# Two output tiles of the first pointwise layer beside the channel steps, in a one-core conformer trunk

## The chip, the core and the metric

The kernel runs on one core of one Trainium2 chip. The metric is the device time of one execution in microseconds (us); the median of three runs stands for a kernel. A separate execution, recorded by the hardware profiler, gives the profile. Engines are named as the profile does: PE is the matrix engine (PEld its weight loads), DVE the vector engine, ACT the scalar engine, POOL the general one, SP the engine that issues the DMAs.

## The reference

With depth 1 the trunk is one conformer layer and one gated conv-FFN for 1024 positions of width 1024, in float32:

```python
mod = silu(c) @ mod_w + mod_b                       # six vectors of 1024
sh_m, sc_m, gt_m, sh_f, sc_f, gt_f = split(mod, 6)
h = rmsnorm(x, norm_pre_mix) * (1 + sc_m) + sh_m
a, gt = split(h @ a_pw1_w + a_pw1_b, 2)             # pointwise 1
u = causal_dwconv(a * sigmoid(gt), a_dw_w) + a_dw_b # 31 taps
u = silu(layernorm(u)) 
y = u @ a_pw2_w + a_pw2_b
x = x + gt_m * rmsnorm(y, norm_post_mix)
...                                                 # the gated conv-FFN
```

## The kernel before

Positions are cut into two blocks of 512, channels into eight tiles of 128 (k for input channels, j for output channels). Every product of pointwise 1 is made from operands split into a high and a low part: `split` writes the high part (ACT, or DVE) and then the low part (DVE, or POOL), and `mm3` (lines 257 to 259) multiplies high by high, high by low and low by high. So one step of one k on one output tile is six matmuls of 512 columns, three for each of the two halves of the gated unit, and an output tile is 48.

The start of the program (lines 757 to 776) works in this order. `load_norm(0)` loads the four 128-row tiles of the first block of x, squares each on ACT (line 283), takes the root on POOL and scales on DVE (line 285). `pw1_weights(0, DV)` loads the two weight tiles of output tile 0 and splits them. `channel_vectors(k)` loads the 16 tiles of 512 KB of the modulation weights (`mod_ch`), two for each k. Then the loop over k runs four things, one step apart: `channel_partials` (line 150, eight small matmuls a chunk against silu(c), then a copy on ACT at line 154), `channel_sums` (line 159, then two small DVE operations that give the shift and scale of channel tile k), `modulate_T` (four transposes at line 266, the modulation on ACT at line 268, the split on DVE), and `pw1_step` of the k before, for output tile 0 alone. `glu` and the first tap of `conv` close tile 0. Output tiles 1 to 7 follow as whole tiles (`pw1`), each from hT, the eight modulated tiles that stay in SBUF. `load_norm(1)`, the second block of x, stands behind tile 1, and `modulate_block`, its eight times four transposes, behind tile 2.

What sets the order: each engine runs a fixed list in order, which a scheduler makes at build time from the program and from its own estimate of times. Loads go out on SP in its list's order, and at most eight are under way. Buffers are few and rotate: three `raw` tiles for loaded weights, four `W` tiles for split weights, eight `Y` tiles, six PSUM banks (`bank`) and two more (`cbank`) that the channel partials and the convolution share. A transfer or an operation that reuses a buffer waits for its last reader.

Of the kernel before, what the change touches and what calls it, by code (L numbers as in the profile page):

```python
# [8 lines left out]
F32 = mybir.dt.float32  # L9
F32R = mybir.dt.float32r  # L10
AF = mybir.ActivationFunctionType
ALU = mybir.AluOpType
# [3 lines left out]
P = 128  # L16
# [3 lines left out]
KD = D // P  # L20
# [27 lines left out]
def trunk_kernel(ctx, tc, x, vec, rows, mod_ch, mod_hp, w1, w2, wup, wdn, out):  # L48
# [19 lines left out]
    def nm(s):  # L68
        uid[0] += 1
        return f"{s}_{uid[0]}"  # L70

    def bank():
        return ps.tile([P, 512], F32, tag="bank", name=nm("bank"))
# [7 lines left out]
    def tAf():  # L81
        return pa.tile([P, 2, 512], F32, tag="A", name=nm("Af"))
# [7 lines left out]
    def tY():  # L90
        return py.tile([P, 1024], F32, tag="Y", name=nm("Y"))
# [8 lines left out]
    def V(name, i, n=1):  # L100
        o = _OFF[name] + i
        return v[:, o:o + n]
# [20 lines left out]

    cz = cst.tile([P, KD, 32], F32, name="cz")
    nc.gpsimd.memset(cz, 0.0)
    nc.scalar.activation(cz[:, :, 0], V("c", 0, KD), AF.Silu)
    sh_m = cst.tile([P, KD], F32, name="sh_m")
    s_m = cst.tile([P, KD], F32, name="s_m")
    sh_f = cst.tile([P, KD], F32, name="sh_f")
# [7 lines left out]
    def channel_vectors(k):  # L137

        ws = []
        for g in range(2):  # L140
            w = tAf().rearrange("p a b -> p (a b)") if k > 1 else tY()
            dma[0] = nc.sync.dma_start(w, mod_ch[k, g])
            ws.append(w)
        return ws
# [100 lines left out]
            hi.tensor_copy(dst[:, 0], src)  # L245
        split_lo[0] = lo.tensor_tensor(dst[:, 1], src, dst[:, 0].bitcast(F32), op=ALU.subtract)  # L246

    def weights(src, lo=nc.gpsimd):
        raw = pr.tile([P, 1024], F32, tag="raw", name=nm("raw"))
        dma[0] = nc.sync.dma_start(raw, src)  # L250
        w = pw.tile([P, 2, 1024], F32R, tag="W", name=nm("W"))
        split(w, raw, lo=lo)
        return w
# [35 lines left out]
    u = [[None] * KD for _ in range(NB)]  # L289
    tail = cst.tile([P, KD, PAD], F32, name="tail")  # L290

    def pw1_weights(j, lo=nc.gpsimd):
        return weights(w1[j], lo), weights(w1[KD + j], lo)

    def pw1_step(bks, ws, h, k):
        sl = slice(k * P, (k + 1) * P)
        for o, w in zip(bks, ws):
            mm3(o, (w[:, 0, sl], w[:, 1, sl]), (h[:, 0], h[:, 1]), k == 0, k == KD - 1)
# [457 lines left out]

    G, DV = nc.gpsimd, nc.vector
    hT = [[None] * KD for _ in range(NB)]
    xs = load_norm(0)
    ws = pw1_weights(0, DV)  # L760
    chunk = [channel_vectors(k) for k in range(KD)]
    issue = ctx.enter_context(ExitStack())
    issue.enter_context(tc.issue_after(dma[0].ins))

    bks = [bank(), bank()]
    part = [channel_partials(chunk[0])]
    for k in range(KD + 1):
        if k + 1 < KD:
            part.append(channel_partials(chunk[k + 1]))
        if k < KD:  # L770
            channel_sums(k, *part[k])
            hT[0][k] = modulate_T(xs, s_m, sh_m, k)
        if k > 0:
            pw1_step(bks, ws, hT[0][k - 1], k - 1)
    glu(0, 0, bks)
    cs0 = [conv(0, 0, POOL_TAPS)]

    loaded, parts = [], []

# [11 lines left out]
            p, h = todo.pop(0)  # L791
            loaded.append((p, h, piece_loads(p, h)))

    for j in range(1, KD):
        ws = pw1_weights(j)
        pw1(0, j, ws)
        if j == 2:
            with tc.issue_after(dma[0].ins):
                b2, g_f = spread(2, "b2"), spread(4, "g_f")
                g_m, early_m, use_m = into_rows(0, 3, "g_m")  # L800
            into = [(early_m, use_m), (None, into_channels(fin_sh)), (None, into_channels(fin_s))]
            todo = [(p, h) for p in range(3) for h in range(2)]
        if j == 1:
            xs = load_norm(1)
        if j == 2:
            hT[1] = modulate_block(xs, s_m, sh_m, nc.scalar, G)
        if j >= KD - 2:
            pieces()
        cs0.append(conv(0, j, POOL_TAPS))
        if j >= SHARED:  # L810
            pw1(1, j, ws)
            if j >= KD - 2:
                pieces()
# [130 lines left out]
```

## Time and profile before

| | us |
|---|---|
| median of three runs | 1091.83 (1091.65 to 1094.43) |
| the profiled execution, whole | 1093.15 |
| its span in the trace | 1091.4 |
| PE busy in it | 1063.2 |
| all other engines | 819.1 (DVE) or less |

The span is the traced part of the profiled execution; 1.75 us lie around it. PE's busy time includes modelled ends of matmuls, so it is read from the distance between starts rather than from the share. The trace rows give the start, the length, the engine, the line and operation, and in brackets how long the engine had been idle and what ended that. In the first 60 us the loads keep the DMA engines busy from about 5 us to 50 us.

### The profile page before, as it was taken

Reading aid. Unit: us, or ns where it says so; the run is one execution under the profiler, and the core shown is the slowest. Engines: PE = TensorE matmul, PEld = TensorE weight load, DVE = VectorE, ACT = ScalarE, POOL = GpSimd, SP = SyncE. Lnnn points to the kernel's source line nnn. Section 1 sums busy time; section 2 is a strip of 40 time slices with the busy share of each in tenths; the row PEclk is TensorE's granted clock in tenths of the full one; section 3 lists DMA queues with packets and bytes.
Section 4 is the critical chain, followed back from the end, with each engine's and each line's share of the span. In section 5 each row is a group of like instructions: output and inputs, shape, how many; then the busy total and the mean of one; then the engine's idle time right before and its main releaser. Section 6 shows DMA issues by size and latency. Waiting matters only on the chain.

```text
span 1091.4 us, 13051 instructions
## 1 busy us (share of the span) xinstructions
PE 1063.2 (97%) x4786; PEld 842.1 (77%) x4786; DVE 819.1 (75%) x1111; ACT 500.3 (46%) x774; POOL 515.5 (47%) x412
## 2 busy tenths in 40 slices
PE   5999999999899999999999999999999999999996
PEld 3778876778688888888887688888887888878884
DVE  3489989533799999989987683786587456965588
ACT  3495455452644544333444442445445344443443
POOL 1398876534734444444444453423247023650464
PEclk9999999999899999999999999999999999999998
DMA  9951135433422233342243343567214322033122
GB/s 367 374 189 63 41 134 193 155 127 106 145 71 93 96 97 97 97 174 92 97 140 115 96 144 92 179 201 281 91 37 154 116 97 91 19 122 117 39 75 80
DMA packets 41832, 139.01 MB, mean 127 GB/s; under 512 B 4644, under 2 KB 4644, under 8 KB 41768
## 3 DMA queue, kind: packets, MB, share of 16 engines
q1 hardware_dynamic: 41768, 138.18, 37.1%
q8 instruction: 37, 0.61, 0.2%
q14 instruction: 27, 0.22, 0.1%
HBM read 129.77 MB, written 8.39 MB: 127 GB/s over the span
## 4 chain that ended last, share of the span: by engine, by line
PE 85%; DVE 7%; POOL 2%; ACT 2%; issue 2%; DMA 1%; SPq 0%; DVEq 0%; ACTq 0%; POOLq 0%
PE bank L257 26%; PE bank L258 25%; PE bank L259 25%; DVE W L246 1%; DVE R L692 1%; PE bank L629 1%; PE bank L630 1%; PE bank L628 1%; PE bank L266 1%; PE bank L179 1%; DMA Y<-in_mod_ch 1%; DVE Y L474 1%; ACT W L243 1%; PE cbank L150 1%; DVE yacc L657 1%
## 5 line engine op out<-in xcount | busy, mean ns | idle before, releaser
L257 PE MATMUL bank<-A,W 128*128 128x512 f32 x960 | 378.8, 397 | 0.3 <-ACT U L268 0.3
L258 PE MATMUL bank<-A,W 128*128 128x512 f32 x960 | 378.5, 395 | 0.0
L259 PE MATMUL bank<-A,W 128*128 128x512 f32 x960 | 378.2, 395 | 0.0
L246 POOL TENSOR_TENSOR W<-raw,W 128x1024 fp32r<-128x1024 f32 x99 | 242.6, 2452 | 273.1 <-ACT W L243 231.1
L354 DVE SCALAR_TENSOR_TENSOR cbank<-U,vecs,cbank 128x512 f32<-128x512 f32 x424 | 290.8, 749 | 8.8 <-ACT cbank L342 7.6
L257 PEld LDWEIGHTS bank<-A,W 128*128 128x128 f32 x960 | 180.7, 189 | 48.1 <-DVE cbank L354 1.7
L259 PEld LDWEIGHTS bank<-A,W 128*128 128x128 f32 x960 | 180.8, 188 | 43.0 <-issue 0.8
L258 PEld LDWEIGHTS bank<-A,W 128*128 128x128 f32 x960 | 180.9, 188 | 42.7 <-issue 1.1
L243 ACT ACTIVATE W<-raw 128x1024 fp32r<-128x1024 f32 x150 | 158.0, 1054 | 109.7 <-PE bank L259 72.4
L527 ACT ACTIVATE U<-bank,vecs 128x512 f32<-128x512 f32 x88 | 68.4, 778 | 192.3 <-PE bank L259 191.9
L528 DVE SCALAR_TENSOR_TENSOR U<-bank,vecs,U 128x511 f32<-128x511 f32 x88 | 65.4, 745 | 78.5 <-ACT U L527 78.3
L257 PE MATMUL bank<-W,A 128*128 128x512 f32 x304 | 121.1, 398 | 0.0
L258 PE MATMUL bank<-W,A 128*128 128x512 f32 x304 | 120.1, 395 | 0.0
L259 PE MATMUL bank<-W,A 128*128 128x512 f32 x304 | 119.0, 395 | 0.0
L533 POOL TENSOR_TENSOR U<-U,hv 128x2 f32<-128x2 f32 x44 | 13.7, 312 | 154.6 <-DVE U L528 151.7
L246 DVE TENSOR_TENSOR W<-raw,W 128x1024 fp32r<-128x1024 f32 x51 | 62.2, 1221 | 16.3 <-ACT W L243 16.3
L246 DVE TENSOR_TENSOR A<-U,A 128x512 fp32r<-128x512 f32 x73 | 67.2, 932 | 8.2 <-ACT A L243 7.7
L352 POOL TENSOR_TENSOR Q<-Q,Q 128x512 f32<-128x512 f32 x48 | 62.2, 1296 | 15.9 <-ACT Q L348 14.9
L257 PEld LDWEIGHTS bank<-W,A 128*128 128x128 f32 x304 | 57.3, 188 | 13.6 <-DVE U L537 0.2
L258 PEld LDWEIGHTS bank<-W,A 128*128 128x128 f32 x304 | 57.3, 188 | 13.5 <-issue 0.5
L259 PEld LDWEIGHTS bank<-W,A 128*128 128x128 f32 x304 | 57.3, 188 | 13.3
L529 DVE SCALAR_TENSOR_TENSOR U<-bank,vecs,U 128x510 f32<-128x510 f32 x88 | 65.3, 744 | 1.6
(149 smaller groups left out, 1204.1 us busy)
## 6 DMA issues: line engine op xcount, KB each, us to landing
raw<-in_wup SPq DMA_DIRECT2D x88, 512.0 KB, 3.2
raw<-in_w SPq DMA_DIRECT2D x40, 512.0 KB, 3.9
Y<-in_mod_hp SPq DMA_DIRECT2D x32, 512.0 KB, 6.5
raw<-in_wdn SPq DMA_DIRECT2D x22, 512.0 KB, 3.6
R<-in_wdn SPq DMA_DIRECT2D x20, 512.0 KB, 3.6
Af<-in_mod_ch SPq DMA_DIRECT2D x12, 512.0 KB, 10.2
Y<-in_x SPq DMA_DIRECT2D x8, 512.0 KB, 10.0
U<-in_x SPq DMA_DIRECT2D x16, 256.0 KB, 3.8
```

The lines of the kernel that those rows point to most:

```text
L150: nc.tensor.matmul(bk[32 * q:32 * q + 32, 0:256], cz[:, 4 * g + q], ws[g][:, 256 * q:256 * (q + 1)], start=g == 0, stop=g == 1)
L243: nc.scalar.activation(dst[:, 0], src, AF.Copy)
L246: split_lo[0] = lo.tensor_tensor(dst[:, 1], src, dst[:, 0].bitcast(F32), op=ALU.subtract)
L257: nc.tensor.matmul(o, l[0], r[0], start=start, stop=False)
L258: nc.tensor.matmul(o, l[0], r[1], start=False, stop=False)
L259: nc.tensor.matmul(o, l[1], r[0], start=False, stop=stop)
L352: nc.gpsimd.tensor_tensor(acp, acp, q, op=ALU.add)
L354: nc.vector.scalar_tensor_tensor(acc, ut[:, k:k + 512], tap(k), acc, op0=ALU.mult, op1=ALU.add)
L527: nc.scalar.activation(t[:, :512], bk, AF.Identity, bias=V("fb", i), scale=wk[2])
L528: nc.vector.scalar_tensor_tensor(t[:, 1:512], bk[:, 0:511], wk[1], t[:, 1:512], op0=ALU.mult, op1=ALU.add)
L529: nc.vector.scalar_tensor_tensor(t[:, 2:512], bk[:, 0:510], wk[0], t[:, 2:512], op0=ALU.mult, op1=ALU.add)
L533: nc.gpsimd.tensor_tensor(t[:, 0:2], t[:, 0:2], hv[:, g, jj, :], op=ALU.add)
```

## The change

Five edits at the start of the program:

- silu(c) is made as sigmoid on ACT and a product on DVE, where it was one silu on ACT.
- Chunk 0 of the modulation weights is loaded ahead of x; chunk 1 comes behind the weights of output tile 1.
- The weights of output tile 1 are loaded at the start, into two `Y` tiles in place of `raw` tiles, and split with the low part on POOL.
- In the loop, `channel_sums` and `modulate_T` of k stand ahead of `channel_partials` of k + 1, and `pw1_step` runs for output tiles 0 and 1.
- `glu` and the first tap come for tiles 0 and 1 together, then `load_norm(1)`; the loop over whole tiles begins at 2.

```diff
-    nc.scalar.activation(cz[:, :, 0], V("c", 0, KD), AF.Silu)
+    sg_c = cst.tile([P, KD], F32, name="sg_c")
+    nc.scalar.activation(sg_c, V("c", 0, KD), AF.Sigmoid)
+    nc.vector.tensor_tensor(cz[:, :, 0], sg_c, V("c", 0, KD), op=ALU.mult)
...
-            w = tAf().rearrange("p a b -> p (a b)") if k > 1 else tY()
+            w = tAf().rearrange("p a b -> p (a b)") if k > 0 else tY()
...
-        raw = pr.tile([P, 1024], F32, tag="raw", name=nm("raw"))
+        if raw is None:
+            raw = pr.tile([P, 1024], F32, tag="raw", name=nm("raw"))
...
+    chunk = [channel_vectors(0)]
     xs = load_norm(0)
-    ws = pw1_weights(0, DV)
-    chunk = [channel_vectors(k) for k in range(KD)]
+    ws = [pw1_weights(0, DV)]
+    chunk.append(channel_vectors(1))
+    ws.append(pw1_weights(1, raw=tY))
+    chunk += [channel_vectors(k) for k in range(2, KD)]
...
-    bks = [bank(), bank()]
+    bks = [[bank(), bank()] for _ in range(2)]
     part = [channel_partials(chunk[0])]
     for k in range(KD + 1):
-        if k + 1 < KD:
-            part.append(channel_partials(chunk[k + 1]))
         if k < KD:
             channel_sums(k, *part[k])
             hT[0][k] = modulate_T(xs, s_m, sh_m, k)
+        if k + 1 < KD:
+            part.append(channel_partials(chunk[k + 1]))
         if k > 0:
-            pw1_step(bks, ws, hT[0][k - 1], k - 1)
-    glu(0, 0, bks)
-    cs0 = [conv(0, 0, POOL_TAPS)]
+            for j in range(2):
+                pw1_step(bks[j], ws[j], hT[0][k - 1], k - 1)
+    cs0 = []
+    for j in range(2):
+        glu(0, j, bks[j])
+        cs0.append(conv(0, j, POOL_TAPS))
+    xs = load_norm(1)
...
-    for j in range(1, KD):
+    for j in range(2, KD):
...
-        if j == 1:
-            xs = load_norm(1)
```

How the built order moves. PE's list, from the start of the program to the first matmuls of pointwise 1. Names: `Y_122` to `Y_128` are x before, `Y_164` to `Af_174` the modulation chunks 0 to 2, `A_231` the first modulated tile, `bank_196` and `bank_197` output tile 0. Before:

```order
L266 MATMUL bank_224<-ident,Y_128 128x128
L266 MATMUL bank_249<-ident,Y_128 128x128
L150 MATMUL cbank_198<-Y_164,cz 32x256 x4
L150 MATMUL cbank_198<-Y_166,cz 32x256 x4
L150 MATMUL cbank_209<-Y_168,cz 32x256 x4
L159 MATMUL cbank_198<-ones,U_207 128x1 x2
L150 MATMUL cbank_209<-Y_170,cz 32x256 x4
L150 MATMUL cbank_234<-Af_172,cz 32x256 x4
L159 MATMUL cbank_209<-ones,U_218 128x1 x2
L150 MATMUL cbank_234<-Af_174,cz 32x256 x4
L257 MATMUL bank_196<-A_231,W_156 128x512
L257 MATMUL bank_197<-A_231,W_161 128x512
```

The same place after the change, where lines 153, 162, 261 and 270 are the old 150, 159, 257 and 266, `Y_124` and `Y_126` are chunk 0, `Y_128` to `Y_134` are x, and `bank_208` to `bank_211` are output tiles 0 and 1:

```order
L153 MATMUL cbank_212<-Y_124,cz 32x256 x4
L153 MATMUL cbank_212<-Y_126,cz 32x256 x4
L162 MATMUL cbank_212<-ones,U_221 128x1 x2
L270 MATMUL bank_227<-ident,Y_128 128x128
...
L270 MATMUL bank_252<-ident,Y_134 128x128
L261 MATMUL bank_208<-A_234,W_162 128x512
L261 MATMUL bank_209<-A_234,W_167 128x512
L261 MATMUL bank_210<-A_234,W_176 128x512
L261 MATMUL bank_211<-A_234,W_181 128x512
```

Of the small matmuls only chunk 0 is left ahead of the first matmul of pointwise 1; chunks 1 and 2 come behind it.

ACT's list around the first weights of output tile 2. Before, `W_556` and `W_561` are those weights, `Af_547` is the junk output of the last square of the second block of x, and `U_446` the sigmoid of tile 0; the sigmoid of tile 1 comes further behind:

```order
L268 ACTIVATE U_429<-bank_424,sh_m,s_m 128x512
L283 ACTIVATE Af_529,n_90_528<-Y_520 128x1024
...
L283 ACTIVATE Af_547,n_96_546<-Y_526 128x1024
L243 ACTIVATE W_556<-raw_554 128x1024
L303 ACT_TABLE_LOAD
L303 ACTIVATE U_446<-bank_197,vecs 128x512
L243 ACTIVATE W_561<-raw_559 128x1024
```

After, `W_558` and `W_563` are those weights, `U_479` the last modulated tile of the first block, `U_508` and `U_516` the sigmoids of tiles 0 and 1:

```order
L272 ACTIVATE U_479<-bank_474,sh_m,s_m 128x512
L287 ACTIVATE Af_533,n_91_532<-Y_524 128x1024
...
L287 ACTIVATE Af_551,n_97_550<-Y_530 128x1024
L246 ACTIVATE W_558<-raw_556 128x1024
L307 ACTIVATE U_508<-bank_209,vecs 128x512
L246 ACTIVATE W_563<-raw_561 128x1024
L246 ACTIVATE W_712<-raw_710 128x1024
L307 ACTIVATE U_516<-bank_211,vecs 128x512
```

The table load has gone and a third weight tile stands ahead of the second sigmoid.

PE's list at the end of the two tiles. Before, output tile 1 (`bank_465`) ends it, with 17 matmuls behind the last that needs the first weight tile `W_156`, and `bank_564` and `bank_565` are output tile 2:

```order
L259 MATMUL bank_196<-A_431,W_156 128x512
L258 MATMUL bank_197<-A_431,W_161 128x512
...
L259 MATMUL bank_465<-A_431,W_461 128x512
L257 MATMUL bank_564<-A_231,W_556 128x512
L258 MATMUL bank_564<-A_231,W_556 128x512
L257 MATMUL bank_565<-A_231,W_561 128x512
```

After, with `cbank_447` the sums of the last channel tile, `A_444` and `A_481` the last two modulated tiles, and `bank_566` and `bank_567` output tile 2:

```order
L162 MATMUL cbank_447<-ones,U_456 128x1 x2
L261 MATMUL bank_208<-A_444,W_162 128x512
...
L263 MATMUL bank_208<-A_481,W_162 128x512
...
L263 MATMUL bank_211<-A_481,W_181 128x512
L261 MATMUL bank_566<-A_234,W_558 128x512
L262 MATMUL bank_566<-A_234,W_558 128x512
L261 MATMUL bank_567<-A_234,W_563 128x512
```

Between the last sums and output tile 2 there are now 24 matmuls where there were 49, and the first weight buffer comes free six matmuls ahead of their end.

## Rows read from the trace of the kernel before

**Rows 1.** The page's part 1: busy us, share of the span, instructions.
```profile
PE 1063.2 (97%) x4786; PEld 842.1 (77%) x4786; DVE 819.1 (75%) x1111; ACT 500.3 (46%) x774; POOL 515.5 (47%) x412
```

**Rows 2.** Windows: stretch, length, busy by engine, granted clock, DMA share, GB/s.
```profile
10.00:15.00 5.00, 2.85 (x14) 1.07 (x14) 3.57 (x5) 3.40 (x6) 2.05 (x4) 1.00 1.03 419
...
45.00:50.00 5.00, 5.00 (x25) 4.17 (x24) 2.10 (x5) 3.46 (x6) 1.26 (x3) 1.00 1.02 415
```

**Rows 3.** Timeline, ACT and DVE: x, the first weights, the first modulated tile.
```profile
7.68 1.06 ACT L283 ACTIVATE Af<-Y 128x1024 f32<-128x1024 f32 x1 [1.52 <-DMA Y<-in_x]
...
12.72 0.75 DVE L285 TENSOR_SCALAR Y<-Y,n 128x1024 f32<-128x1024 f32 x1 [0.72 <-POOL n L119]
...
13.39 2.35 DVE L246 TENSOR_TENSOR W<-raw,W 128x1024 fp32r<-128x1024 f32 x2
...
19.94 0.78 ACT L268 ACTIVATE U<-bank,sh_m,s_m 128x512 f32<-128x512 f32 x1
...
20.75 0.43 DVE L245 CAST A<-U 128x512 fp32r<-128x512 f32 x1 [1.77 <-ACT U L268]
```

**Rows 4.** Timeline, PE, up to the first matmuls of pointwise 1.
```profile
13.53 0.69 PE L266 MATMUL bank<-ident,Y 128*128 128x128 f32 x2 [0.78 <-DVE Y L285]
...
22.34 1.22 PE L257 MATMUL bank<-A,W 128*128 128x512 f32 x2
23.36 2.76 PE L266 MATMUL bank<-ident,Y 128*128 128x128 f32 x12
25.77 0.61 PE L258 MATMUL bank<-A,W 128*128 128x512 f32 x1
26.22 0.39 PE L259 MATMUL bank<-A,W 128*128 128x512 f32 x1
26.45 0.40 PE L258 MATMUL bank<-A,W 128*128 128x512 f32 x1
```

**Rows 5.** Timeline, PE, one channel step at full pace.
```profile
33.81 1.07 PE L150 MATMUL cbank<-Af,cz 128*32 128x256 f32 x16
34.81 0.61 PE L159 MATMUL cbank<-ones,U 128*128 128x1 f32 x4
35.28 0.64 PE L266 MATMUL bank<-ident,Y 128*128 128x128 f32 x4
35.67 0.71 PE L257 MATMUL bank<-A,W 128*128 128x512 f32 x2
```

**Rows 6.** Windows, as in rows 2, after a gap on PE much later.
```profile
295.00:300.00 5.00, 4.18 (x19) 3.77 (x19) 3.59 (x6) 3.65 (x7) 3.09 (x2) 0.59 0.23 75
```

**Rows 7.** Timeline, PE and ACT, from the last channel sums to output tile 2.
```profile
45.69 0.50 PE L159 MATMUL cbank<-ones,U 128*128 128x1 f32 x4
...
46.54 0.78 ACT L268 ACTIVATE U<-bank,sh_m,s_m 128x512 f32<-128x512 f32 x1 [3.09 <-DVE s_m L161]
...
50.34 1.05 ACT L283 ACTIVATE Af<-Y 128x1024 f32<-128x1024 f32 x1
...
53.78 1.06 ACT L243 ACTIVATE W<-raw 128x1024 fp32r<-128x1024 f32 x1 [2.30 <-PE bank L259]
...
54.85 1.28 ACT L303 ACT_TABLE_LOAD   x1
...
56.15 0.69 ACT L303 ACTIVATE U<-bank,vecs 128x512 f32<-128x512 f32 x1
...
57.52 0.39 PE L257 MATMUL bank<-A,W 128*128 128x512 f32 x1
```

**Rows 8.** Timeline, PE, transposes of the second block behind output tile 2.
```profile
69.55 3.63 PE L266 MATMUL bank<-ident,Y 128*128 128x128 f32 x24
73.45 0.50 PE L257 MATMUL bank<-A,W 128*128 128x512 f32 x1 [0.27 <-ACT U L268]
```

**Rows 9.** Timeline, DVE and PE, end of the first block's convolution.
```profile
202.08 0.69 DVE L356 TENSOR_TENSOR U<-cbank,Q 128x512 f32<-128x512 f32 x1
...
209.76 1.97 PE L373 MATMUL bank<-ident,U 128*128 128x128 f32 x16
```

More of the change, by code (lines that the diff above doesn't have):

```diff
@@ L246, in split, with weights @@
         split_lo[0] = lo.tensor_tensor(dst[:, 1], src, dst[:, 0].bitcast(F32), op=ALU.subtract)
-    def weights(src, lo=nc.gpsimd):
-        raw = pr.tile([P, 1024], F32, tag="raw", name=nm("raw"))
+    def weights(src, lo=nc.gpsimd, raw=None):
+        if raw is None:
+            raw = pr.tile([P, 1024], F32, tag="raw", name=nm("raw"))
         dma[0] = nc.sync.dma_start(raw, src)
@@ L290, in trunk_kernel, with pw1_weights @@
     tail = cst.tile([P, KD, PAD], F32, name="tail")
-    def pw1_weights(j, lo=nc.gpsimd):
-        return weights(w1[j], lo), weights(w1[KD + j], lo)
+    def pw1_weights(j, lo=nc.gpsimd, raw=lambda: None):
+        return weights(w1[j], lo, raw()), weights(w1[KD + j], lo, raw())
     def pw1_step(bks, ws, h, k):
```

## The prediction

> **What bounds the kernel now.** The page's part 1 comes first: PE is busy for 97% of the span, DVE next at 75% [rows 1]. So a change helps only where PE stands idle, waits, or runs below its full pace; PE's list has the same matmuls after the change. The change touches the first 75 us, so the windows and the timeline of that stretch come next.
>
> Two limits meet there. The loads: at 10 to 15 us and still at 45 to 50 us the DMA engines are full, at 419 and 415 GB/s [rows 2], so a tile of 512 KB (0.524 MB) takes about 1.26 us, and what is put ahead in SP's list pushes all behind it. ACT stands idle for the second tile of x until it lands [rows 3]. PE: its first matmuls of pointwise 1 start at 22.34 us [rows 4], output tile 2 at 57.52 [rows 7], and between these two PE has work in order almost without a gap. At full pace a channel step costs 1.00 us for the partials (33.81 to 34.81), 0.47 for the sums and 0.39 for four transposes [rows 5]; a matmul of pointwise 1 costs 0.23 (26.22 to 26.45) [rows 4].
>
> At the start PE is below that pace. The twelve transposes from 23.36 take 2.41 us, 0.20 each [rows 4], where four take 0.39 later [rows 5]; the two matmuls at 25.77 and 26.22 are 0.45 apart [rows 4]. That is the lower of its two clock levels (1.2 and 2.4 GHz), though the clock column says 1.00 at 10 to 15 us [rows 2]; much later, after a gap on PE, the column does show it, with 0.59 for a stretch that mixes both [rows 6]. Since the next pair is 0.23 apart, PE left the lower level at about 26.0, 3.7 us after its first pointwise matmul. Those 3.7 us did 1.85 us of work.
>
> **The change part by part.** I ask when output tile 2 starts on PE, and what then waits.
>
> (a) *Chunk 0 ahead of x.* Two tiles more stand ahead of x, so all that x sets off comes 2.5 us later: DVE's last scaling from 12.72 to 15.2, the two low parts of the first weights from 13.39 to 15.9 with 2.35 us, so to 18.25 [rows 3]. The last transposes of x end at 13.53 + 2.5 + 0.69 = 16.7 [rows 4], and the modulation (0.78) then at 17.5, since chunk 0's partials and sums are done by about 10; before, the modulation stood behind them until 19.94 [rows 3]. So DVE is last: cast from 18.25, 0.43 long, first pointwise matmul at about 18.9. That is 3.4 us earlier. Bounds: 4.1 if the low parts of the weights were not in the way (17.5 + 0.43 + 0.2), 3.0 if x came half a microsecond later than counted.
>
> The page on DMA speaks against this step. The Trainium skill ("DMA: Bandwidth & Descriptors", Specifications) puts the HBM limit of one core at about 358 GB/s. The windows show 415 to 419 [rows 2], so the trace does not agree and the trace decides; by the page, as an estimate, the 3.4 MB up to x's last tile would take 9.5 us in place of 8.2, and the sum below would be 1.3 higher.
>
> (b) *Work put behind the first matmul.* Before, the partials of chunks 0 to 2 and the sums of 0 and 1 were done by 22.34; now only chunk 0 is. Two partials and one sum come after: 2 x 1.00 + 0.47 = +2.5 us of PE time [rows 5]. They lay in time in which PE had to wait anyway. The other chunks land later by two tiles too, but PE reaches them later still.
>
> (c) *A wait for a convolution bank.* Partials of chunk 3 need the bank of chunk 1, which DVE reads after that chunk's sums; in the new list they stand right behind those sums. Sums to modulation took 0.85 us (45.69 to 46.54) [rows 7], of which 0.47 is the sums' own time: +0.4, bounds 0 and 0.85. From there on PE is the slower one, each step's chain having a whole group of 12 matmuls to hide in.
>
> (d) *The clock.* If PE again leaves the lower level 3.7 us after the first pointwise matmul, nothing changes. Before, PE had small matmuls to do ahead of it; now it stands idle from 16.7 to 18.9, so it may take longer. Upper bound: twice as long, +1.85. Lower: full pace from the start, -1.85. I take +0.5, nearer to the repeat, which is the same kind of work.
>
> The skill's page "TensorE: Matmul & The Clock Gate" (Part 1) adds that the number of slow matmuls at the start differs from run to run of one kernel (6, 11 or 14 there). One execution here cannot show it; by it the term would scatter by about a microsecond to either side, and the sum by as much.
>
> So tile 2 could start at -3.4 + 2.5 + 0.4 + 0.5 = 0.0 against 57.52: the earlier start is spent.
>
> (e) *The new wait: ACT's list ahead of tile 2.* Before, the last modulation was at 46.54, the four squares of the second block of x ended at 50.34 + 1.05 = 51.4, and the high part of tile 2's first weights waited until 53.78 for a weight buffer, then 3.7 us were left to PE's 57.52 [rows 7]. The 49 matmuls that stood behind the last sums, most of them tile 1's, covered that. Now only 24 stand there: 24 x 0.23 + 0.47 = 6.0 us from the last sums to tile 2. ACT's chain from the same sums: 51.4 - 45.69 = 5.7 us to the end of the squares, then 1.06 for the high part of the first weights, about 0.65 for the sigmoid of tile 0, 1.05 for the second weights: 8.4 us [rows 7]. PE wants the second weights 0.46 after tile 2's start, at 6.5. So it waits 8.4 - 6.5 = +1.95 us. The weight buffer itself is free 1.2 us ahead of tile 2's start, so it is not last. Queued behind on ACT: a third weight tile, the second sigmoid and the first taps of both convolutions; on PE, all of tile 2. Bounds: 0 if the squares were done earlier than the list says, 2.7 if one more modulation (0.78) lay ahead.
>
> *Silu by sigmoid.* The product on DVE hides in the wait for chunk 0. It takes away the table load of 1.28 at 54.85 [rows 7]; off the path before, it would now stand in the chain of (e), which I counted without it. So 0 against before.
>
> (f) *Transposes of the second block.* Before, 24 of them took 73.45 - 69.55 = 3.9 us, 2.4 of work (0.098 each, [rows 5]) and 1.5 of waits for banks that ACT frees [rows 8]. Now five are taken in the middle of tile 2, 19 at its end, and the banks are freed by the same sigmoid and modulations. I take +0.2 for the second switch; bounds -1.5 (all waits gone) and +0.8 (one more modulation).
>
> (g) *Convolution.* DVE's taps begin behind the second sigmoid, about 4 us later than before. DVE ended the convolution of the first block at 202.8, PE's transposes of it began at 209.76 [rows 9]: 7 us of cover. Cost 0; without that cover the rest would be paid in full.
>
> **Sum:** 0.0 + 1.95 + 0.2 = +2.15 us, rounded 2.2. On the profiled execution, 1093.15 (span 1091.4 and 1.75 around it), that is 1095.3; it stood 1.3 above the median of the runs, so the median goes from 1091.83 to **1094.0**, 0.2% more. What a measurement here can tell from no change is about 0.3%, 3.3 us: below 1088.5 or above 1095.1.
>
> **The rivals.** *The start is kept:* PE at full pace from its first pointwise matmul, (d) at -1.85. For it: PE has done small work from 5 us on. Against: before, 8 us of small matmuls ahead of 22.34 did not do it [rows 4]. Sum -0.2, 1091.6.
>
> *Slower: the lower clock lasts.* (d) at its upper bound: PE idles just before its dense work. Each microsecond more on the lower level costs 0.5; from 2.2 to beyond 3.3 it needs 2.2 us more than I took, so PE would be at the lower level until about 25.8. At the bound: +3.5, 1095.3. For it: the idle stretch 16.7 to 18.9; against: the dense work of twelve transposes and few matmuls raised the clock within 3.7 us [rows 4].
>
> *No wait on ACT:* (e) at 0, the rest as forecast: +0.2, 1092.0. It needs the squares to end 2 us earlier after the sums than 5.7; their list and lengths speak against it.
>
> *Everything pays:* (d) -1.85, (e) 0, (f) -1.5: -3.85, 1088.0. The only way to a gain beyond 0.3%, and it needs three lower bounds at once.
>
> *Loads slower at the start:* chunk 0 and x land one tile's 1.26 us later than counted, and the first matmul with them: +3.4, 1095.2. Against it: the rate has been above 410 GB/s all along [rows 2]. The rule of the Trainium skill's DMA page, above, would make this case.
>
> **How the numbers follow.** Forecast 0.47, start kept 0.16, lower clock 0.20, no wait on ACT 0.08, everything pays 0.06, loads 0.03. Slower by over 0.3%: of the lower clock 0.14, of the forecast's own spread 0.07, loads 0.03, so 0.24. Faster: 0.06 and 0.01 of spread, 0.07. The rest, 0.69, is within. The range leaves out "everything pays" and the top of the clock case: 1090.3 to 1096.5, the ends being -1.5 and +4.7.
>
> **What would show it.** In the profile after: first pointwise matmul near 18.9; pairs of them 0.45 apart until 22.6 or later; tile 2's first matmul near 57.5; then PE idle for about 2 us on the high part of the second weights, named as a wait for ACT, with the four squares just ahead of that in ACT's list; 24 transposes in two pieces. The prediction is wrong if ACT is done with the squares well ahead of tile 2, if tile 2 starts outside 55.5 to 59.5, or if a loss appears behind 75 us that the convolution's cover should have held.

## The result: slower by 0.7%, lost behind the two output tiles

The changed kernel takes 1100.55 us in the median of five runs (1100.05 to 1101.43), the kernel before 1092.07 beside it: a ratio of 1.0071, with a 95% interval of 1.006 to 1.0082. The forecast was +2.2 us with the range ending at 1096.5; measured is +8.5. The profiled execution took 1100.13 us (span 1098.3), 7.0 more than the profiled one of before; the traces account for these 7.0, since the traced execution of before lies 1.1 above its median and that of after 0.4 below. Single runs of the kernel before lay between 1090.97 and 1095.15 over all sets, but for one of 1760.41 at a granted clock of 0.56, which no comparison uses, so ratios are those within one set of runs.

Lines of the changed kernel: 153, 162, 246, 249, 261, 270, 287, 289 and 307 are the old 150, 159, 243, 246, 257, 266, 283, 285 and 303. Timeline of the changed kernel, PE, first matmuls of pointwise 1, the bank of chunk 3, and the end of the two tiles (start us, length, engine, line, operation, in brackets the idle time before it and what ended it):

```profile
18.74 2.07 PE L261 MATMUL bank<-A,W 128*128 128x512 f32 x4 [1.91 <-DVE A L248]
22.61 0.59 PE L262 MATMUL bank<-A,W 128*128 128x512 f32 x1
23.04 0.39 PE L263 MATMUL bank<-A,W 128*128 128x512 f32 x1
27.62 1.07 PE L153 MATMUL cbank<-Af,cz 128*32 128x256 f32 x16 [0.49 <-PE cbank L162]
57.51 0.40 PE L263 MATMUL bank<-A,W 128*128 128x512 f32 x1
```

These answer to [rows 4, 7]. The first matmul is 3.6 us earlier than before, and the two tiles end at 57.51 + 0.23 = 57.74, where the kernel before began tile 2 at 57.52: +0.22. So far the change costs next to nothing. Then, same kernel, ACT, DVE and POOL:

```profile
53.38 1.05 ACT L287 ACTIVATE Af<-Y 128x1024 f32<-128x1024 f32 x1
...
57.55 1.04 ACT L246 ACTIVATE W<-raw 128x1024 fp32r<-128x1024 f32 x1
58.50 0.67 ACT L307 ACTIVATE U<-bank,vecs 128x512 f32<-128x512 f32 x1
59.07 2.00 ACT L246 ACTIVATE W<-raw 128x1024 fp32r<-128x1024 f32 x2
...
58.46 0.76 DVE L289 TENSOR_SCALAR Y<-Y,n 128x1024 f32<-128x1024 f32 x1 [0.77 <-POOL n L119]
59.94 2.85 DVE L289 TENSOR_SCALAR Y<-Y,n 128x1024 f32<-128x1024 f32 x1 [0.72 <-POOL n L119]
...
59.87 2.37 POOL L249 TENSOR_TENSOR W<-raw,W 128x1024 fp32r<-128x1024 f32 x1
```

and PE from there:

```profile
58.65 0.50 PE L261 MATMUL bank<-A,W 128*128 128x512 f32 x1 [0.73 <-ACT W L246]
60.16 0.64 PE L261 MATMUL bank<-A,W 128*128 128x512 f32 x1 [0.78 <-ACT W L246]
61.02 0.84 PE L270 MATMUL bank<-ident,Y 128*128 128x128 f32 x3
62.84 0.47 PE L270 MATMUL bank<-ident,Y 128*128 128x128 f32 x1 [0.98 <-DVE Y L289]
63.50 1.11 PE L270 MATMUL bank<-ident,Y 128*128 128x128 f32 x4 [0.19 <-DVE U L315]
66.12 0.63 PE L261 MATMUL bank<-A,W 128*128 128x512 f32 x1
66.55 0.63 PE L262 MATMUL bank<-A,W 128*128 128x512 f32 x1
67.32 0.39 PE L261 MATMUL bank<-A,W 128*128 128x512 f32 x1
67.55 0.40 PE L262 MATMUL bank<-A,W 128*128 128x512 f32 x1
```

PE waits for tile 2's two weights behind ACT's four squares, then for x, whose fourth scaling took 2.85 us where the other three took 0.75, then for a bank. And from 60.16 to 66.98 its matmuls stand 0.43 us apart. The windows show why (columns: window, then length and busy time of PE, PEld, DVE, ACT, POOL, then the granted clock, DMA share and GB/s):

```profile
58.00:60.00 2.00, 0.74 (x2) 0.30 (x2) 0.82 (x2) 2.00 (x3) 1.83 (x5) 1.00 0.23 94
60.00:62.00 2.00, 1.70 (x5) 0.99 (x5) 2.00 (x1) 1.63 (x3) 2.00 (x1) 0.60 0.00 0
62.00:64.00 2.00, 0.97 (x4) 0.68 (x5) 2.00 (x3) 0.52 (x2) 2.00 (x2) 0.50 0.31 94
```

0.50 is 1.2 GHz. The kernel before shows no such stretch at this place: its clock is 1.00 in every window from 56 to 76 us.

Where the time went, as the lag of the same matmul behind the kernel before: +0.22 at the end of the two tiles; +1.96 through the two waits for weights (60.16 against 57.98); about +1.7 through the waits for x and the bank, by the distances between starts (1.2 and 0.5 us more than the transposes before them need at 1.2 GHz); about +2.5 from 60.2 to 67.3 at 1.2 GHz; -0.2 in the second piece of the transposes. That is +6.1 at the transposes of the first block, 215.84 against 209.76 [rows 9], and it does not change from 80 us to 290. The last 0.9 come later, in steps from 295 us on, and they scatter from run to run (below).

### The profile page after: what moved, and what is told of

The parts are those of the page before. It is cut to its first block, busy times and chain, and to the rows that moved or that the text cites. A ratio compares the mean times of both kernels' runs of the same rounds, so it can differ in the third digit from the quotient of the medians.

```text
span 1098.3 us, 13066 instructions
## 1 busy us (share of the span) xinstructions
PE 1066.1 (97%) x4786; PEld 841.4 (77%) x4786; DVE 820.7 (75%) x1112; ACT 497.8 (45%) x773; POOL 520.9 (47%) x412
## 4 chain that ended last, share of the span: by engine, by line
PE 89%; DVE 5%; POOL 1%; ACT 1%; DMA 1%; issue 1%; SPq 0%; DVEq 0%; ACTq 0%; POOLq 0%
PE bank L261 26%; PE bank L263 26%; PE bank L262 26%; PE bank L633 2%; PE bank L634 2%; PE bank L632 2%; PE bank L270 1%; DVE W L249 1%; PE bank L182 1%; DVE Y L478 1%; DMA Y<-in_x 1%; PE cbank L153 1%; DVE R L696 1%; DVE yacc L661 1%; DMA x2d<-Y 0%
## 5 line engine op out<-in xcount | busy, mean ns | idle before, releaser
L246 ACT ACTIVATE W<-raw 128x1024 fp32r<-128x1024 f32 x148 | 155.8, 1054 | 110.6 <-PE bank L263 68.7
```

Source lines behind the costliest of these rows:

```text
L246: nc.scalar.activation(dst[:, 0], src, AF.Copy)
```

## The experiments

Theory: the loss lies between the end of the two tiles and 80 us, in the lists of ACT and DVE and in what the waits do to PE's clock. Rivals: the four weight buffers that two tiles hold; the second tile or the new order of the start as such; a low clock that has nothing to do with the waits.

One measure serves for all runs: the **growth**, the lag at the transposes of rows 9 less the lag at the end of the two tiles (start of tile 2 in the kernel before: 57.52). It leaves out what happened at the start.

| run | median us | ratio to the kernel before, 95% | end of two tiles | growth |
|---|---|---|---|---|
| changed | 1100.55 | 1.0071 (1.006 to 1.0082) | 57.74 | 5.86 |
| changed again | 1100.15 | 1.0071 (1.0059 to 1.0083) | 56.96 | 5.72 |
| squares early | 1096.93 | 1.0034 (1.002 to 1.0047) | 58.73 | 0.78 |
| squares early, weights first | 1097.03 | 1.0037 (1.0021 to 1.0053) | 59.00 | 0.69 |
| wait filled, 22 matmuls | 1100.31 | 1.0065 (1.0049 to 1.0081) | 59.13 | 5.08 |
| half filled, 12 | 1099.27 | 1.0061 (1.0048 to 1.0074) | 57.82 | 4.10 |
| low parts on DVE | 1097.0 | 1.0037 (1.0024 to 1.005) | 57.59 | 3.16 |
| lists mended | 1095.5 | 1.0023 (1.0015 to 1.0032) | 59.08 | 0.87 |
| one tile along | 1094.89 | 1.0015 (1.0007 to 1.0024) | | |

### The squares out of the way

```diff
     for k in range(KD + 1):
+        if k == 5:
+            xs1 = load_norm(1)
...
-    xs = load_norm(1)
+    xs = xs1
```

> The changed kernel, with the second block's loads of x, squares and scaling called in the sixth channel step and not behind the two output tiles; nothing is left out. On ScalarE three of the four squares then stand ahead of the seventh modulation and one behind the last, so tile 2's first weight copy has one square of 1.05 us ahead of it and not four. Theory (ScalarE's queue): the copy starts when its buffer is free, near 56.5 us and not at 57.55; tile 2's second weight still has a sigmoid ahead of it, so TensorE waits about 1.0 us and not 1.96; x is scaled long before, so the 1.7 us of waits before the transposes go; with the shorter wait TensorE's granted clock stays at 1.00 from 60 to 68 us. The lag behind the kernel before at the thirteenth matmul of tile 2 is then +1.2 us instead of +6.4, and the time 1094 to 1095 us. Rival (weight buffers: four held by two tiles make tile 2 wait): the copies still start after the tiles' last matmuls, the wait stays near 2 us, the time stays at 1099 us or above. Rival (the clock falls whatever the wait): about 1097 us.

The second run has `ws2 = pw1_weights(2)` ahead of the two `glu` as well.

> As the run with the squares in the sixth channel step, and tile 2's weights are also loaded and copied ahead of the gate of tile 0, so that no sigmoid stands between its two copies on ScalarE; nothing is left out. Theory (ScalarE's queue): the copies end near 57.5 and 58.5 us, TensorE's wait for weights falls to about 0.3 us; the gate of tile 0 comes about 1 us later, and the second group of transposes waits about 0.6 us for its bank instead. Lag +0.5 to +1.2 us, time 1093 to 1094.5 us. Rival (weight buffers): 1099 us or above, as without it. Rival (the clock falls whatever the wait): about 1096.5 us.

Growth fell from 5.86 to 0.78 and 0.69, and the clock stayed at 1.00 from 56 us to 290. But the times, 1096.93 and 1097.03, miss what was expected (at most 1095 and 1094.5), because the two tiles ended about 1 us later, and because in these traces the lag grew by another 0.9 to 1.4 us behind 290 us. With the squares early, ACT, DVE and PE:

```profile
49.24 0.78 ACT L272 ACTIVATE U<-bank,sh_m,s_m 128x512 f32<-128x512 f32 x1 [1.41 <-DVE s_m L164]
...
51.77 0.21 DVE L164 SCALAR_TENSOR_TENSOR s_m<-cbank,scb,vecs 128x1 f32<-128x1 f32 x1
51.90 0.42 DVE L248 CAST A<-U 128x512 fp32r<-128x512 f32 x1
...
52.37 1.20 PE L261 MATMUL bank<-A,W 128*128 128x512 f32 x4 [0.78 <-DVE A L248]
```

The cast of step 6 stands behind the channel sums of step 7 in the built list and starts at 51.90; its input was modulated by 50.0. PE waits 0.78 us for it and 0.40 for the low part behind it. A part of the loss, about 1.2 us, was moved from ACT's list to DVE's. On ACT the first weight copy now starts when its buffer comes free:

```profile
57.53 1.06 ACT L246 ACTIVATE W<-raw 128x1024 fp32r<-128x1024 f32 x1 [3.63 <-PE bank L263]
```

That is 1.2 us ahead of the end of the tiles at 58.73. In the changed kernel the same point was 57.74 - 1.2 = 56.5, and the copy started at 57.55. With the squares early, the second weights still cost 1.0 us. So about half of the 1.96 us is the squares, the other half the buffer and the sigmoid between the copies. The weight-buffer rival is right for that half, and wrong as the cause of the loss. With the weights first, the wait for the second weights fell to 0.21 us, as expected, but the transposes behind it took 0.4 us longer than in the kernel before.

### The wait filled with matmuls

```diff
+    def fill(b):
+        with tc.issue_after(lastmm[0].ins):
+            for _ in range(22):
+                nc.tensor.matmul(b, w1hi[:, 0, :P], hT[0][KD - 1][:, 0], start=True, stop=True)
```

called on the first bank of tile 2; the second run has 12.

> The changed kernel with 22 matmuls of 512 columns more on TensorE, between the last matmul of the two output tiles and the first of tile 2; they write a bank of tile 2 that its first real matmul overwrites, so nothing is left out. All waits stay where they are on the other engines (weights ready at 60.1, x scaled at 62.8, bank free at 63.5 us), only TensorE is busy through them: 22 of 0.23 us, from 57.7 to about 62.8. Theory (the waits pull the granted clock down, and the low clock costs 2.5 us by itself): the clock stays at 1.00 from 60 to 68 us; the lag at the ninth matmul of tile 2 is about +5.4 us as against +5.0, but it stays +5.4 where the changed kernel goes on to +6.4; the time is 0.5 to 1.5 us below the changed kernel's 1100.5, though 5 us of matmuls were added. Rival (the clock falls for another reason, such as what the other engines draw there): the lag grows to +8, and the time is 1102 us or above. Rival (the clock costs nothing, since other engines set the pace there): about 1101.5 us.

> The changed kernel with 12 matmuls of 512 columns more ahead of tile 2, not 22; they write a bank that the first real matmul overwrites, so nothing is left out. TensorE is busy through the two waits for weights (57.7 to 60.5 us), but not through the wait for the scaled x (61.4 to 62.8). In the changed kernel the granted clock was down from 60.4 us on, before the wait for x began. If the two waits for weights bring it down: it stays at 1.00, the lag at the ninth matmul of tile 2 is +5.0 us and stays so, and the time is 0.5 to 1.5 us below the changed kernel. If the wait for x does: the clock is down for about 7 us from near 64, and the time is 1 to 2 us above the changed kernel.

PE with 22:

```profile
59.13 5.28 PE L808 MATMUL bank<-A,W 128*128 128x512 f32 x22
64.24 0.39 PE L261 MATMUL bank<-A,W 128*128 128x512 f32 x1
```

and the window behind it:

```profile
64.00:66.00 2.00, 2.00 (x15) 1.72 (x13) 1.69 (x4) 1.09 (x3) 2.00 (x1) 1.00 0.66 213
```

64.24 - 59.13 = 5.11 us of matmuls that nobody needs were added, and the growth is 5.08, 0.6 to 0.8 less than without them: the clock stayed up. The expected gain in time did not show: the median, 1100.31, is that of the changed kernel, and this run's tiles ended 1.4 us later, at 59.13. With 12, PE waited 0.91 us for x all the same:

```profile
62.95 0.33 PE L270 MATMUL bank<-ident,Y 128*128 128x128 f32 x1 [0.91 <-DVE Y L289]
```

and its windows show the clock at 1.00 all the same:

```profile
62.00:64.00 2.00, 0.76 (x6) 0.54 (x6) 2.00 (x3) 0.42 (x2) 2.00 (x2) 1.00 0.34 80
64.00:66.00 2.00, 2.00 (x12) 1.65 (x11) 1.65 (x3) 2.00 (x4) 2.00 (x2) 1.00 0.50 186
```

The growth is 4.10, the time 0.9 us below the changed kernel's in the same set, as expected, though the intervals overlap. In this trace the wait for x alone did not bring the clock down; with the waits for weights filled, 1.6 us of growth went, though 2.8 us of matmuls were added.

### Low parts on DVE

```diff
-        ws = pw1_weights(j)
+        ws = pw1_weights(j, DV if j == 2 else G)
```

> The changed kernel with the low parts of tile 2's two weights made on VectorE and not on GpSimd; nothing is left out. It shows the fourth scaling of x (2.85 us where the other three took 0.75) without a GpSimd subtraction beside it. Theory (the two engines slow each other while both work on 1024-column operands): the scaling takes 0.75 us and ends near 60.7; the first group of transposes then stands ready at once. The bank of the second group still comes from VectorE's gating of tile 0, now behind a low part, so the end moves little: 1099 to 1101.5 us. Rival (the scaling waits for something of its own, such as its scale from GpSimd): it still takes 2.8 us.

DVE and POOL of this run:

```profile
59.80 0.76 DVE L289 TENSOR_SCALAR Y<-Y,n 128x1024 f32<-128x1024 f32 x1 [0.72 <-POOL n L119]
60.47 1.22 DVE L249 TENSOR_TENSOR W<-raw,W 128x1024 fp32r<-128x1024 f32 x1
62.26 2.77 DVE L249 TENSOR_TENSOR W<-raw,W 128x1024 fp32r<-128x1024 f32 x1
...
60.98 2.96 POOL L249 TENSOR_TENSOR W<-raw,W 128x1024 fp32r<-128x1024 f32 x1 [1.22 <-ACT W L246]
```

With POOL idle the scaling takes 0.76 us; the rival falls. The next DVE operation with two inputs takes 1.22 alone and 2.77 beside POOL's. The end moved more than expected: PE was ready for the transposes at 60.6, and the clock stayed at 1.00 with the same two waits of 0.73 and 0.79 us for weights. I expected 1099 or more and got 1097; the bank of the second transposes, on which I had counted, was asked for later, since the scheduler put four transposes there and not eight. Part of the gain is the clock, and may belong to the traced execution alone: its mean clock over the whole run is 0.994, that of the other four 0.992 or 0.993.

### The lists mended

In this run two squares go behind the last partial copy, two behind the last modulation, the scalings behind DVE's last split, tile 2's weights ahead of `glu`:

```diff
+        if k in (6, 7):
+            with tc.issue_after(act[0].ins):
+                scale += [norm(xt) for xt in xs1[2 * (k - 6):2 * (k - 5)]]
...
+    with tc.issue_after(split_lo[0].ins):
+        for f in scale:
+            f()
+    ws2 = pw1_weights(2)
```

> The changed kernel with the three lists behind the two output tiles written out: two squares of the second x block stand behind the last copy of partial sums on ScalarE and two behind the last modulation; tile 2's two weight copies stand ahead of the gate of tile 0; the four scalings of x stand on VectorE behind the last split of the channel steps, so none is ahead of a split (in the runs with the squares in the sixth step, one was, and cost the last step about 1.2 us) and none is beside a GpSimd subtraction. Nothing is left out. Theory (the loss sits in the lists of ScalarE and VectorE around tile 2): the two tiles end where they did in the changed kernel, 0.2 us behind the kernel before; the weight copies run from 56.5 to 58.5 us; TensorE waits about 0.3 us for weights and 0.5 us for banks, the clock stays at 1.00; the lag at the transposes of the first block's convolution is +1.0 us where it was +6.1, and the time within 2 us of the kernel before. Rival (two tiles along with the steps cost more than the lists show): the lag stays above +2.5 us.

> The changed kernel once more, on the chip of the three runs beside it, so that they are compared with it there. If what the first trace of it showed holds for every run: a second stretch of low clock near 60 to 67 us, the fourth scaling of x at 2.8 to 2.9 us, and a time 7 to 9 us above the kernel before. If the stretch of low clock was chance: 4 to 6 us above.

ACT, DVE and PE with the lists mended:

```profile
57.89 2.01 ACT L246 ACTIVATE W<-raw 128x1024 fp32r<-128x1024 f32 x2 [0.99 <-PE bank L263]
...
58.88 0.75 DVE L289 TENSOR_SCALAR Y<-Y,n 128x1024 f32<-128x1024 f32 x1 [0.71 <-POOL n L119]
...
59.08 0.42 PE L261 MATMUL bank<-A,W 128*128 128x512 f32 x1
59.95 0.50 PE L261 MATMUL bank<-A,W 128*128 128x512 f32 x1 [0.22 <-ACT W L246]
60.52 1.44 PE L270 MATMUL bank<-ident,Y 128*128 128x128 f32 x8
```

PE goes from the last matmul of tile 1 into tile 2 without a break, loses 0.4 us at the second weights (0.87 between starts, where 0.46 are work) and about 0.6 in the eight transposes, which take 1.40 us where the kernel before needs 0.79. Growth 0.87, where it was 5.7 and 5.9. In the same set of runs that is 1095.5 against 1100.15: two thirds of the loss. The expected time (within 2 us) was missed by a little, 2.3 us and 0.23%, and the lag at the transposes is +2.4 where +1.0 was expected, just short of the rival's +2.5: this run's tiles ended at 59.08, for a reason that lies at the start.

The changed kernel again, 6.9 us above the kernel before, gave the same waits for weights, the scaling of 2.85 us, and a low stretch, but at another place. PE, then the windows:

```profile
62.06 0.33 PE L270 MATMUL bank<-ident,Y 128*128 128x128 f32 x1 [1.62 <-DVE Y L289]
```

```profile
60.00:62.00 2.00, 0.45 (x4) 0.21 (x2) 2.00 (x2) 0.85 (x2) 2.00 (x2) 1.00 0.00 0
62.00:64.00 2.00, 1.60 (x6) 1.39 (x7) 1.69 (x4) 1.30 (x3) 2.00 (x1) 0.64 0.68 229
64.00:66.00 2.00, 2.00 (x6) 1.55 (x5) 1.90 (x3) 2.00 (x5) 2.00 (x2) 0.51 0.52 137
```

Here PE waited for x at full clock, so the wait is 1.62 and not 0.98 us long, and the low stretch came 2 us later and was shorter. The growth is nearly the same. So the split of the loss into "wait for x" and "clock" belongs to one execution; their sum does not. A low stretch itself seems to belong to every run: the mean clock over an execution is 0.991 or 0.992 in all ten of the changed kernel, and 0.993 to 0.995 in the 21 with the squares early or the lists mended.

### One tile along

The three smaller edits (sigmoid, chunk 0 ahead of x, sums ahead of partials), and `pw1_step` for tile 0 alone, `load_norm(1)` behind tile 1 as before:

```diff
...
-            for j in range(2):
+            for j in range(1):
...
```

> The kernel before with all parts of the change but one: sigmoid, the first modulation chunk ahead of x, and the channel sums ahead of the next partials are in, the second output tile along with the steps is not, so the loads of x and its squares stand behind tile 1 as before. Nothing is left out. Theory (only the second tile, by what it does to ScalarE's list, costs time): the first pointwise matmul is near 19 us and not 22.3, the steps end within 1 us of the kernel before, and the time is within 2 us of it. Rival (the order of sums and partials or of the loads costs by itself): 3 us or more slower than the kernel before.

The lag at the transposes of rows 9 is +0.1, and the first pointwise matmul is at 18.26. Without the second tile nearly all the loss is gone; whether through ACT's list alone this run does not say, since it also changes the start:

```profile
16.27 1.97 PE L153 MATMUL cbank<-Af,cz 128*32 128x256 f32 x16
...
54.62 0.39 PE L261 MATMUL bank<-A,W 128*128 128x512 f32 x1
...
69.85 3.31 PE L270 MATMUL bank<-ident,Y 128*128 128x128 f32 x16 [1.94 <-ACT U L307]
```

with a low clock behind it in the windows:

```profile
70.00:72.00 2.00, 1.98 (x12) 1.50 (x12) 2.00 (x4) 2.00 (x4) 2.00 (x2) 0.80 0.24 35
72.00:74.00 2.00, 2.00 (x9) 1.81 (x8) 2.00 (x4) 2.00 (x4) 2.00 (x2) 0.50 0.71 252
```

Tile 2 starts at 54.62, 2.9 us ahead of the kernel before. No weights of tile 1 are loaded ahead of chunk 1, so PE makes its partials at 16.27, where the changed kernel stands idle and makes them from 21.59 on; and the matmuls are at full pace from about 20 us, there from 23. By this trace the three smaller edits do earn something, and the second tile costs about that much at the start. The 2.9 us are lost again at the second block's transposes, where PE waits for ACT's sigmoid and then runs at the low clock. Of the 1.5 us that this trace is slower in the end, 1.3 come behind 290 us.

### The start

In six traces with the changed order of the start, the partials of chunk 3 (27.62 above) come between 26.84 and 29.01 us, and the two tiles end 30.1 us later each time: 27.62 and 57.74, 29.01 and 59.13, 28.96 and 59.08, 27.69 and 57.82, 26.84 and 56.96, 27.49 and 57.59. (With the squares early it is more, for the wait for the cast.) In the kernel before it is 30.50 from 27.02, with one tile along 30.69 from 23.93. PE has the same work left from that point, so an earlier first matmul cannot bring the end forward unless this point moves. It scatters with the first pointwise matmul, which lies between 18.30 and 19.30, and with the clock: matmuls are 0.43 us apart until 25.0 in the two traces where it is late, until 23.0 or less in the others. Two questions: does the order of sums and partials set it, and does the low clock?

```diff
+        if k + 1 < KD:
+            part.append(channel_partials(chunk[k + 1]))
+            ...
         if k < KD:
             channel_sums(k, *part[k])
             hT[0][k] = modulate_T(xs, s_m, sh_m, k)
-        if k + 1 < KD:
-            part.append(channel_partials(chunk[k + 1]))
```

(in the kernel with the lists mended)

> The changed kernel with its lists mended, and one part of the change undone: the next chunk's partial sums again stand ahead of this chunk's sums, as in the kernel before. Nothing is left out. In the mended kernel the second chunk's sums come at 27.9 us, behind a partial that stands behind the matmuls of step 0, and TensorE waits twice 0.5 us around it. If the order of sums and partials costs there: the second sums come near 21 us, these waits go, the two tiles end 0.5 to 1.5 us earlier, and the time is 0.5 to 1.5 us below the mended kernel's (1.0023 of the kernel before). If TensorE's amount of work alone sets the end of the tiles: within 0.5 us of the mended kernel, though the first pointwise matmul comes 1 to 2 us later.

1097.9 us, ratio 1.0039 (1.0026 to 1.0051) against 1.0023 (1.0015 to 1.0032): both readings missed, it is not faster. PE:

```profile
18.80 1.08 PE L153 MATMUL cbank<-Af,cz 128*32 128x256 f32 x8 [2.11 <-DMA Af<-in_mod_ch]
23.33 2.05 PE L261 MATMUL bank<-A,W 128*128 128x512 f32 x4
...
59.58 0.40 PE L261 MATMUL bank<-A,W 128*128 128x512 f32 x1
```

The partials wait for their loads, and the first matmuls of pointwise 1, which were ready, stand behind them. The first matmul comes 4.1 us later for it, but tile 2 only 0.5 us later (59.58 against 59.08), and the lag behind the mended kernel stays 0.5 us until 290 us; the rest of the difference in time comes behind that. So "sums ahead of the next partials" earns about 0.5 us here by the traces, and the times, whose intervals overlap, show no more: it takes a wait for a load out from in front of ready work.

For the clock, matmuls of constants were added where PE idles at the start:

```diff
+    def warm(at, mm=None):
+        n = WARM.pop(at, 0)
+        with tc.issue_after(mm.ins) if mm and n else ExitStack():
+            for _ in range(n):
+                nc.tensor.matmul(bks0[0][:, 0:P], over_d, over_d, start=True, stop=True)
```

> The kernel before with matmuls of constants added on TensorE where it idles in the first 14 us: 24 ahead of the first transposes, 8, 3 and 3 between the transposes of the x tiles; they write a bank that the first real matmul overwrites, so nothing is left out. In the kernel before TensorE is busy without a break from 14.2 us, yet its matmuls of 512 columns stand 0.43 us apart until 26.2 us: the low clock covers all of the start. If the clock at the start is a price of its own (what made the ends of the two tiles scatter by 2 us from run to run in the changed kernel): the clock is up by about 8 us, the partials from 14.2 to 22.3 us take half as long as far as the loads allow, tile 2 starts 1 to 3 us earlier, and the time is 1 to 3 us below the kernel before. Rival (the loads set the pace of the start): no change, within 0.5 us.

> The changed kernel with its lists mended (as in the run of that name) and the same kind of filling: 12 matmuls of constants ahead of the first partial sums, 6 between their halves, 10 behind the first sums, 3, 3 and 8 behind the transposes of the x tiles, all where TensorE idles; nothing is left out. In the mended kernel TensorE is busy from 19.3 us and the clock rises near 25 us. If the low clock there is what keeps the two tiles from ending earlier: the 5.7 us at the low clock shrink to about 3, the partial sums of the fourth chunk come near 26.5 us and not at 28.96, tile 2 starts near 56.5 us, and the time is 1 to 3 us below the mended kernel, within 1.5 us of the kernel before. Rival (the order of partials, sums and transposes sets it, whatever the clock): within 0.5 us of the mended kernel.

> The kernel before with the added matmuls of constants of the run before (24 ahead of the first transposes, 8, 3 and 3 between them) and 9 more, two to four at a time, behind the first two chunks' partial sums and the second channel sums, where the run before still showed TensorE idle for 0.3 to 1.1 us at a time from 14 to 19.4 us; its granted clock fell from 20.5 to 23.9 us behind these gaps. Nothing is left out. If those gaps brought the clock down: it now stays at 1.00 from about 8 us on, tile 2 starts 2.5 to 3.5 us earlier than in the kernel before, and the time is 2 to 3 us below it in the median, not only in single runs. Rival (the loads then set the pace, whatever the clock): within 1 us of the kernel before.

The first gave 1093.56 us, ratio 1.0007 (0.9997 to 1.0016). In its trace, which is of its fastest execution (1090.84), the clock fell again behind the short gaps that were left, as the windows show:

```profile
18.00:20.00 2.00, 0.93 (x13) 0.46 (x12) 1.22 (x4) 0.38 (x1) 0.00 (x0) 1.00 1.03 412
21.00:22.00 1.00, 1.00 (x7) 1.00 (x6) 0.00 (x0) 0.00 (x0) 0.00 (x0) 0.50 1.01 406
```

With these filled too, PE keeps its full pace through the start, by the distances of its matmuls from about 6 us on, the scatter of the runs is about halved (1091.63 to 1093.56), and the time is 1092.63, ratio 0.999 (0.9981 to 0.9999): the fastest kernel of this study, by 0.1%. Of the 2 to 3 us expected it earned 1.2. In its trace tile 2 starts 1.4 us earlier than in the kernel before, and 0.5 of that is lost again at the second block's transposes; what holds the rest back was not settled. On the mended kernel the filling gave 1095.09 (1.0017, 1.0008 to 1.0025), no clear difference from 1.0023, and decides nothing: ten of the added matmuls (20 instructions in the trace) stood ahead of a transpose whose tile was scaled by 13.2 us,

```profile
13.00 4.61 PE L304 MATMUL bank<-over_d 128*128 128x128 f32 x20
17.41 0.64 PE L272 MATMUL bank<-ident,Y 128*128 128x128 f32 x2
```

and pushed it to 17.4; the granted clock fell to 0.50 there all the same, from about 11 to 18 us. A mended version with the filling better placed was not tried.

## Why the prediction was wrong, point by point

- **(a) to (d), the start: right in its terms.** First matmul 18.74 (forecast 18.9), wait for the bank 0.49 (0.4), clock 4.3 us after the first matmul (4.7, since +0.5 stands for 1 us more at the low level), tile 2 due at 57.74 (57.5). But (b) put the later landing of the other chunks at nothing ("PE reaches them later still"). With one tile along, where no weights of tile 1 are loaded ahead of chunk 1, PE makes that chunk's partials before the first matmul and tile 2 starts 2.9 us early: part of the work that (b) counts stands behind the first matmul because chunk 1 lands late. The scatter that I gave to the clock is there: the tiles end between 56.96 and 59.13. The page "TensorE: Matmul & The Clock Gate" (Part 1) of the Trainium skill says that slow matmuls at the start differ in number from run to run; the traces agree (the low pace lasts until 21.9 us in one execution of the changed kernel, until 23.0 in the other).
- **(b) The order of sums and partials was priced by PE's work alone.** It does cost that work, and it takes away a wait for loads, worth about 0.5 us by the traces of the run with partials first.
- **(e) ACT's list: right, to the hundredth by luck.** The two waits of 0.73 and 0.78 us cost 1.96 us from start to start (1.95). The squares end 5.8 us after the last sums (5.7), and the tiles 6.0 us (6.0). But the squares hold only half of the wait: with them out of the way the weight buffer, called "not last", is last, and it and the sigmoid, which (e) did count, hold the other half.
- **(f) is the step that failed.** It counted what the transposes wait for as banks only, and only for the 24 later ones, which came out at -0.2 (forecast +0.2). The loss fell on the eight that stand behind the first four matmuls of tile 2, in both kernels, and in no term. They also need x scaled, and the scaling hangs on the same squares, one root on POOL and one operation on DVE further: 57.55 + 2.4 to 59.94, then 0.75, so 60.7 where PE begins this group at 61.0. That left 0.3 us of cover or little more that I never wrote down, and POOL's low part of tile 2's weights, started 0.07 us ahead, took it: 2.85 us in place of 0.75. About +1.7, forecast 0.
- **(d) stopped at the start, and failed with it.** A low clock after a gap was among the rows [rows 6], and (e) itself forecast 2 us of waiting; the two were not put together, so the price stood at 0. The cost is about 2.5 us in the first trace, less in the second. With the waits filled the clock stayed up, in one trace each; but it also stayed up in the trace with low parts on DVE, where the same two waits for weights were left. So the waits for weights alone do not decide it. Of the 4.8 us between the forecast's +2.2 and the +7.0 of the two traces, (f) and the clock make 4.2.
- **Nothing behind 80 us was to be lost.** The convolution held: +6.08 at its end, as at 80 us. The +0.9 later is not the change: between 232 and 589 us the lag grows by 1.0 here, by 0.0 in the mended kernel, by 1.0 in the kernel before with the most matmuls added, by 0.8 with one tile along, and by 1.8 with partials first. It follows where the low clock near 300 us falls in a gap of PE. That is read from the traces, not tested.

Slower by over 0.3% had a chance of 0.24, most of it for a lower clock at the start; it came from waits behind the start.

## What to carry to other kernels

When work is pulled forward, list what else hangs on the chain that becomes late, down to the last consumer: here the squares fed not only the weights' place in ACT's list but also x. Price a forecast wait on PE twice, once for its length and once for the clock behind it. And look at which engine's list the scheduler puts the moved work into: calling it earlier moved a part of the loss from ACT to DVE, and an order written out removed it there, though not what the second tile costs at the start.

## What the runs showed of the hardware

- Two kinds of DVE operation beside a POOL subtraction of 1024 columns were not slowed in proportion but held up: the scaling of 0.75 us took 2.85 in both traces of the changed kernel and 2.94 with one tile along, the subtraction of 1.22 took 2.77. The Trainium skill ("SBUF — State Buffer", Who interferes with whom) says that the two engines share a pair of ports that one of them holds for a whole instruction while the other waits. The trace agrees: 2.85 us are about 2.1 of waiting and 0.75 of work, POOL's operation, begun 0.07 us earlier, takes 2.37, and POOL's next one, begun while the scaling ran, takes 2.82.
- Two waits of 0.73 and 0.78 us on PE within 2.5 us were followed by a granted clock of 0.50 for 6.8 us in one execution of the changed kernel; in another execution the low stretch came 2 us later, and the trace with low parts on DVE had the same waits and none. When such waits cost clock was not settled.
